# Side-by-side products for head pairs, and another order for the last output blocks, in a two-layer hybrid trunk

## Chip, cores and metric

The kernel runs on one NeuronCore of a Trainium2 chip. The metric is the device time of one launch in microseconds (us), from the first to the last instruction on the chip and what lies around them. Lower is better. Engines are named as in the profile: PE multiplies matrices (PEld is its loading of weights), DVE is the vector engine, ACT the scalar engine, POOL GpSimd, and SP issues the transfers.

## What is computed

Two layers, each on 512 tokens of width 1024. All in float32:

```
x <- x + 1/2 * SwiGLU_1(RMSNorm(x))              # 1024 -> 2 x 2816 -> 1024
h  = RMSNorm(x);  P = h @ W_in
y_A = RWKV-7 time mixing (8 heads of 64, decay and rate from rank-64 products, delta-rule state scan)
y_B = band attention (8 heads of 64, relative-position bias, softmax)
y_C = cross-attention into a memory of 256 tokens (4 heads of 128)
x <- x + W_out( sum_b sigmoid(h W_gate_b + b_gate_b) * (y_b @ W_branch_b) )
x <- x + 1/2 * SwiGLU_2(RMSNorm(x))
```

## The kernel before

Activations lie transposed: 128 channels on the partitions, 512 tokens along the row, so x is eight tiles `xs[0]` to `xs[7]`. A large product takes three half-precision (f16) matmuls for one in float32: weights and activations are split into a high and a low part, and `mm3` (line 714) adds high·high, high·low and low·high in PSUM. Each weight chunk is loaded by SP, measured and split by ACT and DVE (`load_w`, tile `wh`). Small products run in float32 directly; each float32 matmul has two records in the trace, one for each pass of it.

Nothing runs in the order in which it is written. Every operation is recorded (line 538 issues all of them, so all rows of the profile have that line), and `Plan.run` then lays the operations out on PE, DVE, ACT, POOL and SP with estimated costs and hands each engine a fixed order. Work on the longest remaining chain comes first; the f16 sums of large products fill PE between the small ones; matmuls recorded inside one `plan.block()` stay together. `plan.step(True)` makes the next large sum wait for the last one. Where the planner expects PE to stand idle for over 0.4 us it puts in matmuls on a tile of zeros (`xps<-wt`, 320 columns), which are called fills here; they keep PE's clock up, and their result is not used.

A layer has three parts. **First SwiGLU** (`ffn`): 22 blocks of the input projection, then output blocks; of an output chunk, the sums over the first 16 hidden blocks come from weights `w_a(n)` (one chunk of 128 outputs), those over the last 6 from `w_b(c)` (two chunks). `back` adds a sum to its `xs[n]`. For the last pair of chunks the second half of the sums is made for tokens 0 to 255 first, then for 256 to 511 (`HV`), so that the norm of the first half of the tokens, which the next part begins with, can start early. **Mixing** (`mixing`): projections, time mixing (`rwkv`), band attention (`band`), memory attention, gates and branches, and at its end `w_out`, in the last block also by halves. **Second SwiGLU**. A norm squares `xs[0]` to `xs[7]` on ACT, adds them up on DVE, and crosses the partitions by small matmuls (`s<-con,na` for the sum, `s<-con,rs` for the broadcast).

Places that the change touches, where 64-wide heads lie in pairs `u` = 0, 1 on partitions 0 to 63 and 64 to 127 (`H2`; `W2` is the two swapped):

- `soft` in `band`: for each of 4 pairs of heads, 4 blocks `b` of 128 queries and both `u`, a score product with 64 rows of contraction and (b+1)·128 keys (`as<-ak,aq`), into one of two PSUM tiles `a_ps()`; then bias, maximum, exponential and scaling on DVE and ACT, then `turn`, PE transposes of the result (`as<-con,sc`), which take a tile of the same two.
- `rwkv`, the products for decay and rate (`s<-xwa,lw`, 64 rows of contraction, 512 columns), one on each half of the partitions.
- `rwkv`, the output `yp` of each of 8 chunks of 64 tokens: for each `u` one product over 128 rows (`yp<-ar,gx`) and one over 64 (`yp<-kk,g` or `yp<-ta,g`), added in PSUM. This runs for 4 pairs of heads, 8 chunks and 2 layers. Ahead of it in each chunk stands the chain of the state, three pairs of products into `xps` (`xps<-ar,gx`, `xps<-cx,tt`, then `xps<-kk,kb` with `xps<-ta,be`), with DVE or ACT between them.

Of the kernel before, what the change touches and what calls it, by code (L numbers as in the profile page):

```python
# [10 lines left out]
AF = mybir.ActivationFunctionType  # L11
# [5 lines left out]
P = 128  # L17
DM = 1024
T = 512
DEPTH = 2  # L20
KT = DM // P
DFF = 2816
NH = DFF // P
NA = 16
MT = 256
CH = 64
# [529 lines left out]
def trunk(tc: tile.TileContext, i: dict, out: bass.AP, dbg: dict | None = None, depth: int = DEPTH):  # L556
# [47 lines left out]
    def s_ps():  # L604
        return pq.tile([P, T], F32, tag="s", name=nm("s"))

    def a_ps():
        return pa.tile([P, T], F32, tag="a", name=nm("as"))
# [188 lines left out]
    def ffn(l, f, g, d_h, start=(), body=()):  # L797
        start, body = iter(start), iter(body)
        with plan.pool(name=nm("fp"), bufs=30, reuse_waits="tile") as fp:
# [77 lines left out]
                w, d = load_w(i["ffn_outb"][l, f, c], (NH - NA) * 2 * P)  # L877
                return w.rearrange("p s (k n) -> p s k n", k=NH - NA), d

            for c in range(KT // 2):  # L880
                back(*w_a(2 * c), 0, 2 * c, 0, NA, dA)
                a, b = w_a(2 * c + 1), w_b(c)
                for c0, c1 in HV if c == KT // 2 - 1 else ((0, T),):
                    back(*a, 0, 2 * c + 1, 0, NA, dA, c0, c1)
                    for u in range(2):
                        back(*b, u, 2 * c + u, NA, NH, dB, c0, c1)
            plan.step(False)


# [81 lines left out]
    def mixing(l, pieces, kst):  # L971
# [106 lines left out]
        def band():  # L1078
            for p in range(NP):
                q_, k_, vt = att_of[p]  # L1080
                bias = ta_("bias", [P, 2, 2 * P])
                D.dma_start(out=bias, in_=i["bias"][l, p])
                V.memset(bias[0:CH, :, 2 * P - CH:2 * P], -1e30)
                sqs = []
                for t in (k_, q_):
                    sq = ta_("sc", bufs=3)
                    S.activation(sq, t, AF.Square)
                    sqs.append(sq)
                rs = []
                for sq in sqs:  # L1090
                    v = small("n8", 8)
                    V.tensor_scalar(out=v, in0=head_ss(sq, a_ps), scalar1=1.0 / CH, scalar2=1e-6, op0=ALU.mult, op1=ALU.add)
                    rs.append(rpow(v, 8))
                rq = small("rq", 8)
                V.tensor_scalar(out=rq, in0=rs[1], scalar1=CH ** -0.5, scalar2=None, op0=ALU.mult)
                V.scalar_tensor_tensor(out=k_, in0=k_, scalar=lv["aqk"], in1=head_bc(rs[0], a_ps), op0=ALU.mult, op1=ALU.mult)
                pt = []
                for u in range(2):
                    t = ta_("pt", [P, 1280], bufs=2)
                    pt.append([t[:, c0:c0 + T - b * P] for b, c0 in enumerate((0, 512, 896, 1152))])  # L1100

                def soft(b, u):
                    nk = (b + 1) * P
                    h = H2[u]
                    ps = a_ps()
                    PE.matmul(ps[:, :nk], lhsT=q_[h, b * P:(b + 1) * P], rhs=k_[h, 0:nk], start=True, stop=True)
                    sc = ta_("sc", bufs=3)
                    far = max(0, nk - 2 * P)
                    for c0, c1, bb in ((0, far, bias[:, u, 0:1].to_broadcast([P, far])), (far, nk, bias[:, u, 2 * P - (nk - far):2 * P])):
                        if c1 > c0:  # L1110
                            V.scalar_tensor_tensor(out=sc[:, c0:c1], in0=ps[:, c0:c1], scalar=rq[:, 2 * b + u:2 * b + u + 1], in1=bb, op0=ALU.mult, op1=ALU.add)
                    nx = small("nx")
                    V.tensor_reduce(out=nx, in_=sc[:, :nk], op=ALU.max, axis=AX.X, negate=True)
                    den = small("den")
                    S.activation(sc[:, :nk], sc[:, :nk], AF.Exp, bias=nx[:, 0:1], accum_out=den)
                    rd = small("rd")
                    V.reciprocal(rd, den)
                    V.tensor_scalar(out=sc[:, :nk], in0=sc[:, :nk], scalar1=rd[:, 0:1], scalar2=None, op0=ALU.mult)
                    return b, u, sc

                def turn(b, u, sc):
                    ps = a_ps()
                    with plan.block():
                        for kb in range(b + 1):
                            PE.transpose(ps[:, kb * P:(kb + 1) * P], sc[:, kb * P:(kb + 1) * P], ident)
                    for kb in range(b + 1):
                        S.activation(pt[u][kb][:, (b - kb) * P:(b - kb + 1) * P], ps[:, kb * P:(kb + 1) * P], AF.Copy)

                pend = []
                for b in range(4):  # L1130
                    for u in range(2):
                        pend.append(soft(b, u))
                        if len(pend) > 1:
                            turn(*pend.pop(0))
                turn(*pend.pop(0))
                ps = a_ps()
                with plan.block():
                    for kb in range(4):
                        for u in range(2):
                            PE.matmul(ps[H2[u], kb * P:T], lhsT=vt[:, kb, u * CH:(u + 1) * CH], rhs=pt[u][kb], start=(kb == 0), stop=(kb == 3))  # L1140
                y = tm("ya", bufs=5)
                S.activation(y, ps, AF.Copy)
                ya.append(y)
# [91 lines left out]
        def rwkv():  # L1235
            for p in range(NP):
# [14 lines left out]
                else:  # L1251
                    D.dma_start(out=vfs[p], in_=v_)

                ps = s_ps()
                PE.matmul(ps, lhsT=glob["lw"][0:CH, cs], rhs=glob["xwa"][0:CH, :], start=True, stop=True)
                tz = tr("w", bufs=3)
                S.activation(tz, ps, AF.Tanh, scale=0.5, bias=lv["w0"][:, p:p + 1])
                V.tensor_scalar(out=tz, in0=tz, scalar1=1.0, scalar2=None, op0=ALU.add)
                ps = s_ps()
                PE.matmul(ps, lhsT=glob["lw"][CH:P, cs], rhs=glob["xwa"][CH:P, :], start=True, stop=True)  # L1260
                ta = tr("ta")
                S.activation(ta, ps, AF.Tanh, scale=0.5, bias=lv["a0"][:, p:p + 1])
                cu = tr("w", bufs=3)
                V.tensor_tensor_scan(out=cu, data0=con[:, C_CM:C_CM + T], data1=tz, initial=0.0, op0=ALU.mult, op1=ALU.add)

# [111 lines left out]
                for c in range(NCH):  # L1377
# [24 lines left out]
                            else:  # L1402
                                S.activation(z, xp_[w, 2 * CH:3 * CH], AF.Copy, scale=aw[w, c:c + 1])
                    with plan.block():
                        for u, h in enumerate(H2):
                            o, w = yp[h, c * CH:(c + 1) * CH], W2[u]
                            PE.matmul(o, lhsT=gx[:, c, u, CH:2 * CH], rhs=vz[:, c, u, :], start=True, stop=False)
                            PE.matmul(o, lhsT=g1[w, c, :], rhs=vu[u][w, c, :], start=False, stop=True)


# [95 lines left out]
                put(mgd[k], acc[k], s)  # L1506
        for c2 in range(2):
            ws = [chunk(i["w_out"][l, 2 * c2 + c]) for c in range(2)]
            for c0, c1 in HV if c2 else ((0, T),):
                for (k0, k1), dx in zip(groups, dmg):  # L1510
                    for c in range(2):
                        w, d = ws[c]
                        dd = mul_d(d, dx)
                        for u in range(2):
                            n = 4 * c2 + 2 * c + u
                            plan.step(False)
                            ps = g_ps()[:, c0:c1]
                            mm3(ps, [(w[:, 0, k, u * P:(u + 1) * P], w[:, 1, k, u * P:(u + 1) * P], mgd[k][:, 0, c0:c1], mgd[k][:, 1, c0:c1]) for k in range(k0, k1)])
                            x = xs[n][:, c0:c1]
# [158 lines left out]
```

## Time and profile before

| | us |
|---|---|
| median of 3 runs | 2773.04 (2770.26 to 2778.02) |
| the profiled execution | 2773.73 |
| its span, first to last instruction | 2771.9 |
| PE busy | 2745.1 |
| DVE busy | 1626.2 |
| ACT busy | 1538.0 |

The rows further down are of this execution. A timeline row has the start, the length, the engine, the operation with output and inputs, partitions x elements, and how many instructions it merges. PE works in a pipe, so a row's length is longer than the time that it holds PE up; what one group of matmuls costs is the start of the next minus its own start.

### The profile page before, as it was taken

The page shows a single profiled execution, that of the slowest core. Times are in us where ns is not written, and L with a number is a line of the kernel's source. Part 1 is how long each engine was busy: PE and PEld are TensorE (multiplying, and loading weights), DVE is VectorE, ACT ScalarE, POOL GpSimd, SP SyncE. Part 2 cuts the span into 40 slices and gives each one's busy share as a digit, 9 for nine tenths or more (in the row PEclk, how much of TensorE's full clock was granted, in tenths as well). Part 3 has the DMA queues.
Part 4 walks back from the last instruction along what each step waited for, and adds up shares of the span by engine and source line. Part 5 has one row for each costly group of instructions (what it writes and reads, how often), then busy time and mean ns, then how long its engine had stood idle before and what let it go on. Part 6 is the DMA issues. An engine that isn't in the chain of part 4 may idle for free. (4 is left out here: it accounts for less than half of the span.)

```text
span 2771.9 us, 45458 instructions
## 1 busy us (share of the span) xinstructions
PE 2745.1 (99%) x18153; PEld 1496.6 (54%) x18153; DVE 1626.2 (59%) x4391; ACT 1538.0 (55%) x2543; POOL 111.1 (4%) x285
## 2 busy tenths in 40 slices
PE   9999999999999999999999999999999999999999
PEld 6444486565645456444564444765655454654445
DVE  6344486777766676354463544777776666743543
ACT  6556475565645566565455654655655445655652
POOL 0000000000000000000000000000000000000000
PEclk9999999999999999999999999999999999999999
DMA  4222341111121223222222223311212112232332
GB/s 169 105 93 103 122 140 69 51 61 45 52 83 70 85 98 115 95 104 99 99 107 105 93 106 118 129 52 42 70 35 75 67 54 92 92 114 100 107 106 77
DMA packets 47157, 249.36 MB, mean 90 GB/s; under 512 B 5312, under 2 KB 10688, under 8 KB 23648
## 3 DMA queue, kind: packets, MB, share of 16 engines
q1 hardware_dynamic: 46944, 246.45, 25.2%
q8 instruction: 142, 2.33, 0.3%
q14 instruction: 71, 0.58, 0.1%
HBM read 239.09 MB, written 7.34 MB: 89 GB/s over the span
## 5 line engine op out<-in xcount | busy, mean ns | idle before, releaser
L538 PEld LDWEIGHTS <-wh 128*128 128x128 f16 x10920 | 1047.6, 98 | 1008.0 <-issue 26.8
L538 PE MATMUL g<-hh,wh 128*128 128x512 f16 (+1 forms) x3216 | 987.0, 367 | 0.4 <-DVE k L538 0.4
L538 ACT ACTIVATE wh<-wr,qs 128x1024 f16<-128x1024 f32 (+2 forms) x478 | 484.0, 1050 | 222.5 <-PE g L538 114.3
L538 ACT ACTIVATE junk<-wr 128x2048 uint8<-128x2048 f32 (+2 forms) x239 | 412.9, 1727 | 332.9 <-DMA wr<-ffn_in 144.3
L538 PE MATMUL g<-hl,wh 128*128 128x512 f16 (+1 forms) x1608 | 588.9, 366 | 0.0
L538 DVE SCALAR_TENSOR_TENSOR wh<-wr,qs,wh 128x1024 f16<-128x1024 f32 (+2 forms) x478 | 545.2, 1168 | 43.8 <-ACT wh L538 42.9
L538 PE MATMUL as<-hh,wh 128*128 128x512 f16 (+1 forms) x1536 | 443.3, 361 | 0.0
L538 PE MATMUL as<-hl,wh 128*128 128x512 f16 (+1 forms) x768 | 277.4, 361 | 0.0
L538 PE MATMUL as<-ab,wh 128*128 128x512 f16 (+1 forms) x1224 | 234.7, 350 | 0.0
L538 PE MATMUL g<-ab,wh 128*128 128x512 f16 (+1 forms) x1224 | 234.5, 350 | 0.0
L538 POOL PARTITION_ALL_REDUCE ar<-wm x239 | 97.3, 407 | 2465.5 <-ACT junk L538 2313.6
L538 DVE SCALAR_TENSOR_TENSOR a<-as,md,sg 128x512 f32<-128x512 f32 x44 | 33.0, 750 | 213.3 <-PE as L538 210.0
L538 DVE SCALAR_TENSOR_TENSOR a<-g,md,sg 128x512 f32<-128x512 f32 x44 | 33.0, 750 | 212.9 <-PE g L538 202.7
L538 DVE SCALAR_TENSOR_TENSOR x<-g,md,x 128x512 f32<-128x512 f32 (+1 forms) x62 | 39.0, 628 | 115.8 <-PE g L538 115.8
L538 DVE SCALAR_TENSOR_TENSOR x<-as,md,x 128x512 f32<-128x512 f32 (+1 forms) x62 | 38.9, 628 | 115.8 <-PE as L538 115.8
L538 DVE TENSOR_SCALAR qt<-ar 128x1 int32<-128x1 int32 x253 | 37.6, 150 | 104.0 <-POOL ar L538 101.7
L538 ACT ACTIVATE sq<-x 128x256 f32<-128x256 f32 x96 | 37.0, 407 | 78.9 <-DVE x L538 50.6
L538 ACT ACTIVATE kk<-xps 64x64 f32<-64x64 f32 x64 | 14.0, 219 | 112.6 <-DVE ta L538 93.9
L538 ACT ACTIVATE ti<-s 64x256 f32<-64x256 f32 (+1 forms) x144 | 54.3, 378 | 28.2 <-PE s L538 18.3
L538 DVE SCALAR_TENSOR_TENSOR ab<-a,qs,ab 128x512 f16<-128x512 f32 x88 | 60.7, 746 | 10.3 <-ACT ab L538 10.3
L538 ACT ACTIVATE sg<-as,md 128x512 f32<-128x512 f32 x44 | 30.1, 684 | 56.2 <-PE as L538 56.2
L538 ACT ACTIVATE ab<-a,qs 128x512 f16<-128x512 f32 x88 | 55.9, 709 | 7.3 <-DVE qs L538 7.3
(345 smaller groups left out, 3133.4 us busy)
## 6 DMA issues: line engine op xcount, KB each, us to landing
wr<-ffn_in SPq DMA_DIRECT2D x88, 1024.0 KB, 4.8
wr<-ffn_outa SPq DMA_DIRECT2D x32, 1024.0 KB, 4.9
wr<-w_gate SPq DMA_DIRECT2D x24, 1024.0 KB, 4.9
wr<-w_in SPq DMA_DIRECT2D x22, 1024.0 KB, 4.9
wr<-ffn_outb SPq DMA_DIRECT2D x16, 768.0 KB, 4.3
wr<-w_branch SPq DMA_DIRECT2D x24, 512.0 KB, 3.5
wr<-mem_kv SPq DMA_DIRECT2D x8, 1024.0 KB, 4.9
wr<-w_out SPq DMA_DIRECT2D x8, 1024.0 KB, 4.8
```

Source lines behind the costliest of these rows:

```text
L538: f(*[x.real() if isinstance(x, View) else x for x in a], **{y: x.real() if isinstance(x, View) else x for y, x in k.items()})
```

## The change

It does five things. The two score products of a block `b` are recorded together in one `plan.block()`, before both softmaxes, and take both PSUM tiles. The decay and rate products are recorded in one block. In a chunk's output the two products over 128 rows come first, then the two over 64. In the last pair of chunks of SwiGLU's output the sums over the last 6 hidden blocks come first and whole, and then the two sums over the first 16, by halves of the tokens. In the last block of `w_out`, within a half, the sums go chunk by chunk and no longer group by group, and each waits for the last one (`plan.step(c2 == 1)`).

```diff
-            for c in range(KT // 2):
+            for c in range(KT // 2 - 1):
                 back(*w_a(2 * c), 0, 2 * c, 0, NA, dA)
                 a, b = w_a(2 * c + 1), w_b(c)
-                for c0, c1 in HV if c == KT // 2 - 1 else ((0, T),):
-                    back(*a, 0, 2 * c + 1, 0, NA, dA, c0, c1)
-                    for u in range(2):
-                        back(*b, u, 2 * c + u, NA, NH, dB, c0, c1)
+                back(*a, 0, 2 * c + 1, 0, NA, dA)
+                for u in range(2):
+                    back(*b, u, 2 * c + u, NA, NH, dB)
+            c += 1
+            b = w_b(c)
+            for u in range(2):
+                back(*b, u, 2 * c + u, NA, NH, dB)
+            ws = [w_a(2 * c + u) for u in range(2)]
+            for c0, c1 in HV:
+                for u in range(2):
+                    back(*ws[u], 0, 2 * c + u, 0, NA, dA, c0, c1)
...
-                def soft(b, u):
+                def scores(b):
                     nk = (b + 1) * P
-                    h = H2[u]
-                    ps = a_ps()
-                    PE.matmul(ps[:, :nk], lhsT=q_[h, b * P:(b + 1) * P], rhs=k_[h, 0:nk], start=True, stop=True)
+                    pss = [a_ps(), a_ps()]
+                    with plan.block():
+                        for ps, h in zip(pss, H2):
+                            PE.matmul(ps[:, :nk], lhsT=q_[h, b * P:(b + 1) * P], rhs=k_[h, 0:nk], start=True, stop=True)
+                    return pss
...
                 for b in range(4):
+                    pss = scores(b)
                     for u in range(2):
-                        pend.append(soft(b, u))
+                        pend.append(soft(b, u, pss[u]))
...
-                ps = s_ps()
-                PE.matmul(ps, lhsT=glob["lw"][0:CH, cs], rhs=glob["xwa"][0:CH, :], start=True, stop=True)
+                ps, ps2 = s_ps(), s_ps()
+                with plan.block():
+                    PE.matmul(ps, lhsT=glob["lw"][0:CH, cs], rhs=glob["xwa"][0:CH, :], start=True, stop=True)
+                    PE.matmul(ps2, lhsT=glob["lw"][CH:P, cs], rhs=glob["xwa"][CH:P, :], start=True, stop=True)
...
-                        for u, h in enumerate(H2):
-                            o, w = yp[h, c * CH:(c + 1) * CH], W2[u]
+                        ys = [yp[h, c * CH:(c + 1) * CH] for h in H2]
+                        for u, o in enumerate(ys):
                             PE.matmul(o, lhsT=gx[:, c, u, CH:2 * CH], rhs=vz[:, c, u, :], start=True, stop=False)
+                        for u, (o, w) in enumerate(zip(ys, W2)):
                             PE.matmul(o, lhsT=g1[w, c, :], rhs=vu[u][w, c, :], start=False, stop=True)
...
-            for c0, c1 in HV if c2 else ((0, T),):
-                for (k0, k1), dx in zip(groups, dmg):
-                    for c in range(2):
+            order = [(0, T, g, c) for g in range(2) for c in range(2)]
+            if c2:
+                order = [(c0, c1, g, c) for c0, c1 in HV for c in range(2) for g in range(2)]
...
-                            plan.step(False)
+                            plan.step(c2 == 1)
```

Since the planner orders everything anew, the change moves instructions far beyond these lines. Three places on PE, the first of each kind in the program, before and then after.

A chunk's output in `rwkv` of layer 0 (`yp`), with the matmuls next to it. Before:

```order
L538 MATMUL xps<-kk_5163,kb_1014_4121 64x64
L538 MATMUL xps<-ta_5081,be_4783 64x64
L538 MATMUL yp_294<-ar_4769,gx_4124 64x64
L538 MATMUL yp_294<-kk_5163,g_1002_4125 64x64
L538 MATMUL yp_294<-ar_4769,gx_4124 64x64
L538 MATMUL yp_294<-ta_5081,g_1002_4125 64x64
L538 LDWEIGHTS wh_4912
```

The two products of one head stood together, and then those of the other. After:

```order
L538 MATMUL g_5593<-wh_5497,hl_2570 128x128
L538 MATMUL yp_294<-ar_4771,gx_4163 64x64 x2
L538 MATMUL yp_294<-kk_5194,g_1000_4164 64x64
L538 MATMUL yp_294<-ta_5103,g_1000_4164 64x64
L538 LDWEIGHTS hh_2571
```

Now the products of the two heads that have one shape are neighbours.

The scores of the first pair of heads in `band`, layer 0, block b = 1 (`as<-ak,aq`, 256 keys); `g` rows are f16 sums of a projection. Before, with most rows between the two heads left out:

```order
L538 MATMUL g_5188<-wh_5146,hl_2570 128x128
L538 MATMUL as_5305<-ak_4151,aq_4153 128x256
L538 LDWEIGHTS hh_2571
...
L538 MATMUL as_5393<-ak_4151,aq_4153 128x256
L538 MATMUL as_5392<-con,sc_5023 128x128
```

The second head's product came much later than the first's. After:

```order
L538 MATMUL xps<-kk_5194,kb_1012_4160 64x64
L538 MATMUL xps<-ta_5103,be_4785 64x64
L538 MATMUL as_5235<-ak_4190,aq_4192 128x256
L538 MATMUL as_5295<-ak_4190,aq_4192 128x256
L538 MATMUL xps<-ar_4771,gx_4163 64x64 x2
```

Now the two stand next to each other.

The end of `w_out` in layer 0, ahead of the second SwiGLU: `as` and `g` are the last sums, `s<-con,na` crosses the partitions for the norm of a half of the tokens, `s<-con,rs` spreads its result, and `xps<-wt` are fills. Before:

```order
L538 MATMUL s_10173<-con,na_11161 128x1 x2
...
L538 MATMUL s_10185<-con,rs_3747 128x128 x2
...
L538 MATMUL as_11265<-ti_9718,wh_10963 128x256
L538 LDWEIGHTS wt
L538 MATMUL xps<-wt 128x320
...
L538 MATMUL s_11206<-con,na_11363 128x1 x2
```

The first half's two crossings stood among the last sums; 26 fills followed the last sum, then the second half's crossing. After:

```order
L538 MATMUL s_10312<-con,na_11185 128x1 x2
...
L538 MATMUL g_11265<-ti_9831,wh_11039 128x256
L538 LDWEIGHTS wt
L538 MATMUL xps<-wt 128x320
...
L538 MATMUL s_10322<-con,rs_3733 128x128 x2
...
L538 MATMUL s_11296<-con,na_11408 128x1 x2
```

The first half's spread has moved behind the last sum: 28 fills stand ahead of it, and 14 more between it and the second half's crossing.

## Rows read from the trace of the kernel before

**Rows 1.** The page: span, busy time and share of each engine, and the granted TensorE clock in 40 slices (9 is 90% or more).

```profile
span 2771.9 us, 45458 instructions
PE 2745.1 (99%) x18153; PEld 1496.6 (54%) x18153; DVE 1626.2 (59%) x4391; ACT 1538.0 (55%) x2543; POOL 111.1 (4%) x285
PEclk9999999999999999999999999999999999999999
```

**Rows 2.** Busy time of each engine by stage: the stretch, its length, then busy us (instructions) of each engine, granted clock, share of DMA and GB/s. The stretches are mixing of layer 0, its gates and w_out, the two SwiGLUs between, mixing of layer 1.

```profile
430.00:930.00 500.00, 490.83 (x4309) 280.74 (x4306) 350.40 (x1060) 267.25 (x567) 15.61 (x41) 1.00 0.17 60
930.00:1040.00 110.00, 110.00 (x614) 59.89 (x613) 75.28 (x188) 69.73 (x104) 5.96 (x16) 1.00 0.28 101
1040.00:1790.00 750.00, 750.00 (x4048) 396.05 (x4046) 372.13 (x886) 419.96 (x585) 31.62 (x80) 1.00 0.30 107
1790.00:2300.00 510.00, 501.23 (x4348) 284.26 (x4346) 357.97 (x1067) 275.39 (x576) 15.96 (x40) 1.00 0.17 59
```

**Rows 3.** Timeline of PE: the decay and rate products of one pair of heads where they happened to stand together, and one such product alone.

```profile
421.60 1.13 PE L538 MATMUL s<-xwa,lw 64*128 64x512 f32 x4
422.67 0.39 PE L538 MATMUL g<-hh,wh 128*128 128x512 f16 x1
...
542.48 0.38 PE L538 MATMUL g<-hh,wh 128*128 128x512 f16 x1
542.78 1.12 PE L538 MATMUL s<-xwa,lw 64*128 64x512 f32 x2
543.84 0.39 PE L538 MATMUL g<-hh,wh 128*128 128x512 f16 x1
```

**Rows 4.** Timeline of PE: score products of both heads together (128 keys), and of one head alone (256, 384 and 512 keys), each with the row behind it.

```profile
489.24 0.49 PE L538 MATMUL as<-ak,aq 64*128 64x128 f32 x4
489.66 0.28 PE L538 MATMUL g<-wh,hh 128*128 128x128 f16 x2
...
492.36 0.70 PE L538 MATMUL as<-ak,aq 64*128 64x256 f32 x2
492.99 0.29 PE L538 MATMUL g<-wh,hh 128*128 128x128 f16 x2
...
557.91 0.91 PE L538 MATMUL as<-ak,aq 64*128 64x384 f32 x2
558.75 0.39 PE L538 MATMUL g<-hh,wh 128*128 128x512 f16 x1
...
507.09 1.12 PE L538 MATMUL as<-ak,aq 64*128 64x512 f32 x2
508.14 0.44 PE L538 MATMUL as<-con,sc 128*128 128x128 f32 x2
```

**Rows 5.** Timeline of PE: the first record of the last step of a chunk's state chain, the same chunk's output in `rwkv`, and the row behind it.

```profile
496.84 0.27 PE L538 MATMUL xps<-kk,kb 128*64 128x64 f32 x1
...
497.01 0.28 PE L538 MATMUL yp<-ar,gx 128*64 128x64 f32 x2
497.22 0.33 PE L538 MATMUL yp<-kk,g 64*64 64x64 f32 x2
497.48 0.33 PE L538 MATMUL yp<-ar,gx 128*64 128x64 f32 x2
497.74 0.33 PE L538 MATMUL yp<-ta,g 64*64 64x64 f32 x2
497.99 0.28 PE L538 MATMUL g<-wh,hh 128*128 128x128 f16 x2
```

**Rows 6.** Timeline of PE and DVE: two steps of a chunk's state chain, each with both heads' products as neighbours, and the DVE copy between them.

```profile
617.57 0.34 PE L538 MATMUL xps<-ar,gx 128*64 128x64 f32 x4
617.83 1.12 PE L538 MATMUL as<-ak,aq 64*128 64x512 f32 x2
617.95 0.22 DVE L538 COPY cx<-xps 128x64 f32<-128x64 f32 x1
...
618.88 0.33 PE L538 MATMUL xps<-cx,tt 64*64 64x64 f32 x4
619.15 0.39 PE L538 MATMUL g<-hh,wh 128*128 128x512 f16 x1
```

**Rows 7.** Fills: the matmuls on the tile of zeros in all (count, then shortest, median and longest record in ns, first and last start in us, forms), and two groups of them on PE's timeline with the rows behind them; a row of which PE waited for something would end in brackets.

```profile
L538 PE MATMUL xps<-wt x337: 296/299/474, 1.0 to 2439.7; 128*128 128x320 f16 x169
...
1039.43 3.74 PE L538 MATMUL xps<-wt 128*128 128x320 f16 x26
1043.02 0.50 PE L538 MATMUL s<-con,na 128*128 128x1 f32 x4
...
1396.58 2.23 PE L538 MATMUL xps<-wt 128*128 128x320 f16 x15
1398.65 0.27 PE L538 MATMUL g<-hh,wh 128*128 128x256 f16 x1
```

**Rows 8.** Timeline of DVE and ACT: the softmax of one head's block of 128 queries and 512 keys, whose score product ended PE's part at 583.97 us (bias in two pieces, maximum, exponential, scaling).

```profile
584.08 0.88 DVE L538 SCALAR_TENSOR_TENSOR sc<-as,rq,bias 128x256 f32<-128x256 f32 x2 [1.15 <-PE as L538]
...
584.99 0.69 DVE L538 TENSOR_REDUCE nx<-sc 128x1 f32<-128x512 f32 x1
...
585.71 0.72 ACT L538 ACTIVATE sc<-sc,nx 128x512 f32<-128x512 f32 x1 [1.30 <-DVE nx L538]
...
586.77 0.49 DVE L538 TENSOR_SCALAR sc<-sc,rd 128x512 f32<-128x512 f32 x1
```

More of the change, by code (lines that the diff above doesn't have):

```diff
@@ L1100, in band, with soft @@
                     pt.append([t[:, c0:c0 + T - b * P] for b, c0 in enumerate((0, 512, 896, 1152))])
-                def soft(b, u):
+                def scores(b):
                     nk = (b + 1) * P
-                    h = H2[u]
-                    ps = a_ps()
-                    PE.matmul(ps[:, :nk], lhsT=q_[h, b * P:(b + 1) * P], rhs=k_[h, 0:nk], start=True, stop=True)
+                    pss = [a_ps(), a_ps()]
[3 more added lines that the diff above has]
+                    return pss
+                def soft(b, u, ps):
+                    nk = (b + 1) * P
                     sc = ta_("sc", bufs=3)
@@ L1258, in rwkv @@
                 V.tensor_scalar(out=tz, in0=tz, scalar1=1.0, scalar2=None, op0=ALU.add)
-                ps = s_ps()
-                PE.matmul(ps, lhsT=glob["lw"][CH:P, cs], rhs=glob["xwa"][CH:P, :], start=True, stop=True)
                 ta = tr("ta")
-                S.activation(ta, ps, AF.Tanh, scale=0.5, bias=lv["a0"][:, p:p + 1])
+                S.activation(ta, ps2, AF.Tanh, scale=0.5, bias=lv["a0"][:, p:p + 1])
                 cu = tr("w", bufs=3)
@@ L1508, in mixing @@
             ws = [chunk(i["w_out"][l, 2 * c2 + c]) for c in range(2)]
-            for c0, c1 in HV if c2 else ((0, T),):
-                for (k0, k1), dx in zip(groups, dmg):
-                    for c in range(2):
-                        w, d = ws[c]
-                        dd = mul_d(d, dx)
-                        for u in range(2):
+            order = [(0, T, g, c) for g in range(2) for c in range(2)]
+            if c2:
+                order = [(c0, c1, g, c) for c0, c1 in HV for c in range(2) for g in range(2)]
+            for c0, c1, g, c in order:
+                    (k0, k1), dx = groups[g], dmg[g]
+                    w, d = ws[c]
+                    dd = mul_d(d, dx)
+                    for u in range(2):
                             n = 4 * c2 + 2 * c + u
-                            plan.step(False)
+                            plan.step(c2 == 1)
                             ps = g_ps()[:, c0:c1]
```

## The prediction

> **What bounds the kernel now.** I read the page first: PE is busy for 2745.1 of 2771.9 us, at full granted clock in every slice, and DVE and ACT for little over half [rows 1]. So PE's idle time is 26.8 us in all, under 1%. The table by stage says where: gates, w_out and the two SwiGLUs have none, the two mixing stages have 9.2 and 8.8 us [rows 2]. DVE is the next engine there, with 350.4 of 500 us. Nothing can be won by starting PE earlier; what counts is how long its queue is, and that is what the change touches. The sum below is therefore PE's queue, term by term, plus what it waits.
>
> A busy PE isn't a useful one, though: 337 of its matmuls are fills [rows 7], and they belong to the queue too.
>
> **Two products side by side.** A timeline shows what two products cost that use different halves of the partitions. At 421.60 the decay and rate products stand together, four records, and PE goes on 1.07 us later; the one at 542.78 alone takes 1.06 us [rows 3]. Two cost what one costs. In the order of before 2 of 8 such pairs are neighbours already; the other 6 save 6 x 1.06 = **6.4 us**.
>
> Scores: a head alone takes 0.63, 0.84 and 1.05 us for 256, 384 and 512 keys; the two of 128 keys are neighbours already, 0.42 us for both [rows 4], in all 8 pairs of heads (4 in each layer). The other three blocks are apart in all 8. I take the second product as free, as in rows 3: 8 x (0.63 + 0.84 + 1.05) = **20.2 us** saved.
>
> Output of a chunk: now 497.99 - 497.01 = 0.98 us [rows 5]. No row has it in the new order, but rows 6 have both of its halves in form. Two products over 128 rows, into the two halves of PSUM's partitions, take 0.26 us (617.57 to 617.83); two over 64 rows, one on each half, take 0.27 us (618.88 to 619.15). So 0.53 us, 0.45 us less, for 4 x 8 x 2 = 64 chunks: **28.8 us** saved. The ends: a pair that is followed by another of its form holds PE for only 0.17 us (496.84 to 497.01) [rows 5], which would save 0.09 x 64 = 6 us more; and if nothing overlapped, nothing would be saved. I take 0.53, since the second pair has another form than the first, as what follows the pair at 617.57 has.
>
> Together PE's queue gets 55.4 us shorter. Places where PE goes from f16 to float32 work are 477 in the order before and 485 after, so I count nothing for changing over.
>
> **What the new order adds.** The order of after holds 555 fills, 218 more. A fill costs 3.59 us / 26 = 0.138 us at 1039.43 and 2.07 / 15 = 0.138 at 1396.58, and behind neither group does PE wait further [rows 7]; the fills were enough, so each added one is time in the queue, whether the gap it was meant for is real or not: 218 x 0.138 = **30.1 us** added. By place, from the two orders: the start 116 and 116; the norms ahead of and behind the SwiGLUs 87 and 87; the ends of w_out 103 and 151; inside mixing 31 and 201.
>
> That settles the two reorderings of last blocks. For SwiGLU's output the fills stay the same, so I cost it at nothing: it makes 48 more matmuls, each half as wide, and the columns are the same. Its weights come in another order on SP's queue (w_b ahead of the two w_a), and of the two `wh` buffers both are held to the end, as before; the SwiGLU stages have PE at 750.00 of 750.00 us [rows 2], which is the cover. For w_out the new order costs 48 x 0.138 = 6.6 us (in the 30.1): with each sum waiting for the last, xs[2] and xs[3] get their last addend behind the first sums of the last block, the squares of a norm run in the order of xs, and so the first half's norm ends behind the last sum.
>
> **Waits.** PE reaches the next step of a state chain 0.45 us sooner in each chunk. In rows 6 the copy that the second step reads ends at 618.17, and PE gets there at 618.88: 0.71 us, more than it loses. If that held nowhere, 64 x 0.45 = 29 us would come back. In the other direction, the fills that were put in for products costed apart may cover waits that are there now, of which mixing has 18 us; I bound that at -8. I take +3, near the row's end.
>
> **The sum.** 2771.9 - 55.4 + 30.1 + 3 = 2749.6 us of span. The profiled execution is 1.8 us longer than its span, and the median is 0.7 us under it, so **2751 us**, 0.8% faster.
>
> **Rivals.** *The softmaxes fall behind (slower).* A pair of scores takes both `as` tiles. Before, one head's scores could go ahead while the other's transposes held the second tile; now the pair waits on its engine until the last transposes are copied out, and the whole of PE's queue waits behind it. A head's softmax takes from 583.97 to 587.26, 3.3 us [rows 8]. If each of the 24 pairs of over 128 keys leaves PE with 1.5 us of it, that is 36 us, and 2787 us; it decides from 24 / 24 = 1.0 us for each pair. For it: the order of after has fills ahead of transposes and head sums of band and memory attention. Against: between a pair and its first head's transposes that order has 12 to 78 f16 matmuls besides other work, which at the rows' rates is 3 us or more each time, and DVE has 30% of the stage free.
>
> *DVE is late more often.* The same work of 350.4 us in a stage that is 10 to 20 us shorter; PE waits 13 us more than I take, 2764 us.
>
> *The 64-row pair of a chunk's output takes turns.* Both write one PSUM tile, `yp`. If they went one after the other at 0.26 and 0.25 us [rows 5], the block would take 0.77 us and the change would save 0.21 x 64 = 13 us on it: 2766 us. Against it: `xps<-cx,tt` writes one PSUM tile from both halves of the partitions as well, and its four records take 0.27 us [rows 6]. The Trainium skill has this as a rule (TensorEngine Tiling (Array Packing), section Restrictions and Gotchas): different row tiles cannot access the same PSUM bank at the same time. By that rule 2766 us would be right; the trace disagrees with it, with the 0.27 us just named.
>
> *It doesn't do what it says for the outputs.* Accumulating pairs might not overlap at all, since no row has a pair that opens a sum and a second pair that adds to it: 28.8 us less saved, 2780 us.
>
> *More than the forecast.* Fills cover present waits (-8), and the outputs come at 0.44 us (-6): about 2738 us.
>
> **How the numbers follow.** Forecast 0.58; more than it 0.12; DVE late 0.12; taking turns 0.04; no overlap of outputs 0.05; softmaxes behind 0.09. A measurement of this kernel can tell about 0.3% from no change, 8.3 us: faster is under 2764.7, slower over 2781.4. Faster: 0.58 + 0.12 + half of 0.12 = 0.76. Same: the other half, 0.04 and 0.05 = 0.15. Slower: 0.09. The range runs from 2738 to 2770: it leaves out the softmaxes, the outputs without overlap and some 0.05 at the low end.
>
> **What would show it.** Right: `s<-xwa,lw` and `as<-ak,aq` rows of x4 that hold PE for one product's time; a chunk's output in about 0.53 us; 555 fills with no wait behind most groups; mixing some 22 us shorter in layer 0 and 10 in layer 1 (27.7 saved in each, less 44 and 126 fills), and each end of w_out 3 us longer. Wrong: PE idle in mixing well over 18 us, most of all ahead of `as<-ak,aq` or `as<-con,sc` (softmaxes), or ahead of `xps` rows (state chain), or a chunk's output of 0.77 or 0.98 us.

## The result, and the profile after

The changed kernel takes 2755.35 us (median of 4 runs, 2751.40 to 2756.55); the kernel before took 2773.94 us beside it (4 runs, 2770.26 to 2778.02). The ratio is 0.9930 [0.9913, 0.9948], where the brackets hold a 95% interval: 0.7% faster. The forecast was 2751 us. The profiled execution took 2755.16 us.

The page of the changed kernel, with the lines that answer to [rows 1]:

```profile
span 2753.3 us, 45958 instructions
PE 2720.2 (99%) x18419; PEld 1491.8 (54%) x18419; DVE 1621.1 (59%) x4383; ACT 1539.8 (56%) x2543; POOL 111.2 (4%) x285
PEclk9999999999999999999999999999999999999999
```

The span is 18.6 us shorter. PE is busy for 24.9 us less, and its idle time has grown from 26.8 to 33.1 us, so 6.3 us came back as waits. The table by stage of the changed kernel, for the two mixing stages (columns as in [rows 2]; the stretches follow the work, which is earlier now):

```profile
410.00:910.00 500.00, 488.96 (x4442) 278.92 (x4439) 358.14 (x1083) 276.47 (x581) 15.71 (x43) 0.99 0.18 63
1770.00:2275.00 505.00, 490.68 (x4447) 279.30 (x4446) 357.94 (x1078) 280.46 (x584) 17.28 (x43) 1.00 0.17 62
```

The waits are where they were, in mixing: 11.0 and 14.3 us. In layer 0 the granted clock is 0.99 now; it was 1.00.

PE's timeline of the changed kernel at five places: a pair of scores of 512 keys, the end of `w_out` in layer 0, two chunks' outputs, a pair of rate products, and a wait in layer 1 that the order before doesn't have. A bracket is the time that PE stood idle ahead of a row.

```profile
556.64 1.13 PE L538 MATMUL as<-ak,aq 64*128 64x512 f32 x4
557.71 0.39 PE L538 MATMUL g<-hh,wh 128*128 128x512 f16 x1
...
1020.46 4.02 PE L538 MATMUL xps<-wt 128*128 128x320 f16 x28
1024.31 0.60 PE L538 MATMUL s<-con,rs 128*128 128x128 f32 x4
1024.76 2.09 PE L538 MATMUL xps<-wt 128*128 128x320 f16 x14
1026.68 0.50 PE L538 MATMUL s<-con,na 128*128 128x1 f32 x4
1027.05 1.95 PE L538 MATMUL xps<-wt 128*128 128x320 f16 x13
1028.83 0.27 PE L538 MATMUL as<-hh,wh 128*128 128x256 f16 x1
...
1869.54 0.34 PE L538 MATMUL yp<-ar,gx 128*64 128x64 f32 x4
1869.81 0.27 PE L538 MATMUL yp<-kk,g 64*64 64x64 f32 x1
1869.82 0.27 PE L538 MATMUL yp<-ta,g 64*64 64x64 f32 x1
...
1870.07 0.34 PE L538 MATMUL yp<-ar,gx 128*64 128x64 f32 x4
...
2046.49 1.13 PE L538 MATMUL s<-xwa,lw 64*128 64x512 f32 x4
2047.55 1.98 PE L538 MATMUL as<-pt,mv 128*128 128x512 f32 x4
...
2054.19 1.40 PE L538 MATMUL xps<-wt 128*128 128x320 f16 x9
2058.36 0.38 PE L538 MATMUL g<-hh,wh 128*128 128x512 f16 x1 [2.76 <-DVE r L538]
```

Two scores of 512 keys hold PE for 557.71 - 556.64 = 1.07 us, where one alone took 1.05 [rows 4]; two rate products take 1.06. A chunk's output takes 1870.07 - 1869.54 = 0.53 us; the one of [rows 5] took 0.98, and one without a pair of products right ahead of it took 1.03 (rows under "The pairs in the queue"). The two 64-row products that add to `yp` start 0.01 us apart. All these pairs run side by side.

The fills of the changed kernel (columns as in [rows 7]):

```profile
L538 PE MATMUL xps<-wt x555: 296/299/474, 1.0 to 2409.2; 128*128 128x320 f16 x185
```

Where PE's time went can be added up. The table takes, over each whole trace, the time from the start of each PE row to the start of the next, less all time in between in which PE was idle (a bracket shows it where it is over 0.15 us), and adds these times by kind, in us. The last column is the changed kernel with its fills left out (below). The last row is the mean granted clock of the execution.

| PE's time by kind | before | changed | outputs alone | scores alone | three pairs | changed, no fills |
|---|---|---|---|---|---|---|
| waits behind the first matmul | 21.9 | 28.4 | 22.4 | 32.4 | 30.1 | 72.9 |
| fills (count) | 50.9 (337) | 81.9 (555) | 51.0 (337) | 62.3 (422) | 71.2 (476) | 0 |
| chunk outputs | 63.1 | 32.0 | 31.2 | 63.8 | 32.0 | 31.7 |
| scores | 43.8 | 23.9 | 43.8 | 24.4 | 23.8 | 23.8 |
| rate products | 14.7 | 8.9 | 14.7 | 14.7 | 8.5 | 9.8 |
| other float32 | 350.0 | 351.1 | 349.3 | 357.8 | 352.2 | 361.9 |
| f16 | 2222.6 | 2222.5 | 2222.7 | 2226.8 | 2221.5 | 2242.1 |
| mean granted clock | 0.999 | 0.998 | 0.999 | 0.995 | 0.998 | 0.990 |

From before to changed: outputs -31.1, scores -19.9, rates -5.8, fills +31.0, waits +6.5, the rest +1.0; in all -18.3 us.

### The profile page after: what moved, and what is told of

It reads as the page before. It is cut to its first block, busy times and chain, and to the rows that moved or that the text cites. A ratio compares the mean times of both kernels' runs of the same rounds, so it can differ in the third digit from the quotient of the medians.

```text
span 2753.3 us, 45958 instructions
## 1 busy us (share of the span) xinstructions
PE 2720.2 (99%) x18419; PEld 1491.8 (54%) x18419; DVE 1621.1 (59%) x4383; ACT 1539.8 (56%) x2543; POOL 111.2 (4%) x285
## 5 line engine op out<-in xcount | busy, mean ns | idle before, releaser
L538 PEld LDWEIGHTS <-wh 128*128 128x128 f16 x10968 | 1051.7, 98 | 1006.8 <-issue 31.1
L538 PE MATMUL g<-hh,wh 128*128 128x512 f16 (+2 forms) x2704 | 822.5, 365 | 2.8 <-DVE r L538 2.8
L538 PE MATMUL as<-hh,wh 128*128 128x512 f16 (+1 forms) x2048 | 609.2, 366 | 0.1
L538 PE MATMUL g<-hl,wh 128*128 128x512 f16 (+2 forms) x1352 | 492.4, 364 | 0.0
L538 PE MATMUL as<-hl,wh 128*128 128x512 f16 (+1 forms) x1024 | 374.5, 366 | 0.0
L538 DVE SCALAR_TENSOR_TENSOR a<-g,md,sg 128x512 f32<-128x512 f32 x88 | 66.0, 750 | 437.9 <-PE g L538 429.6
L538 ACT ACTIVATE sg<-as,md 128x512 f32<-128x512 f32 x88 | 60.2, 684 | 115.8 <-PE as L538 115.8
L538 PE MATMUL xps<-wt 128*128 128x320 f16 x555 | 88.2, 309 | 1.0 <-DVE wt L538 1.0
L538 PEld LDWEIGHTS <-wt 128*128 128x128 f16 x555 | 55.7, 102 | 26.0 <-issue 1.9
L538 DVE SCALAR_TENSOR_TENSOR ab<-a,qs,ab 128x512 f16<-128x512 f32 x88 | 60.7, 746 | 10.4 <-ACT ab L538 10.4
L538 ACT ACTIVATE pt<-as 128x128 f32<-128x128 f32 (+1 forms) x176 | 42.5, 312 | 39.4 <-PE as L538 38.8
```

What stands on the lines that cost most here:

```text
L538: f(*[x.real() if isinstance(x, View) else x for x in a], **{y: x.real() if isinstance(x, View) else x for y, x in k.items()})
```

## The experiments

Every ratio is against the kernel before, run beside it. The first three take the change apart.

**The outputs alone.** To the kernel before only this was done; the order of all other work and the 337 fills stay as they were:

```diff
-                        for u, h in enumerate(H2):
-                            o, w = yp[h, c * CH:(c + 1) * CH], W2[u]
+                        ys = [yp[h, c * CH:(c + 1) * CH] for h in H2]
+                        for u, o in enumerate(ys):
                             PE.matmul(o, lhsT=gx[:, c, u, CH:2 * CH], rhs=vz[:, c, u, :], start=True, stop=False)
+                        for u, (o, w) in enumerate(zip(ys, W2)):
                             PE.matmul(o, lhsT=g1[w, c, :], rhs=vu[u][w, c, :], start=False, stop=True)
```

> The kernel before with one part alone: in a chunk's output the two products over 128 rows first, then the two over 64. The planner's order and its 337 fills stay as before. Theory (PE's queue sets the time, pairs run side by side): 64 chunks x 0.45 to 0.49 us shorter, 28 to 31 us, so 2743 to 2747 us against 2774. Rival (the state chain takes the time back, PE only waits longer ahead of xps): less than 15 us saved, 2759 us or more.

Measured: 2741.78 us, 0.9888 [0.9872, 0.9905], some 12 us under the changed kernel by the ratios, 13.6 by the times. One of the five edits, without the other four, is the fastest version that was run. PE's timeline of it at the chunk of [rows 5]:

```profile
495.21 0.27 PE L538 MATMUL xps<-kk,kb 128*64 128x64 f32 x1
...
495.38 0.29 PE L538 MATMUL yp<-ar,gx 128*64 128x64 f32 x4
495.60 0.27 PE L538 MATMUL yp<-kk,g 64*64 64x64 f32 x1
...
495.86 0.29 PE L538 MATMUL g<-wh,hh 128*128 128x128 f16 x2
```

Here the output takes 0.48 us, less than 0.53, since it stands right behind a pair of its own form (`xps<-kk,kb` with `xps<-ta,be`). The waits are 22.4 us against 21.9: PE comes to the next step of a state chain half a microsecond earlier, and the step's operands are there.

**All three pairs, without the two orders of last blocks.** The changed kernel, with these two loops put back:

```diff
-            for c in range(KT // 2 - 1):
+            for c in range(KT // 2):
...
-            order = [(0, T, g, c) for g in range(2) for c in range(2)]
...
+            for c0, c1 in HV if c2 else ((0, T),):
...
-                            plan.step(c2 == 1)
+                            plan.step(False)
```

> The changed kernel with both last-block orders undone: only the three pair edits. Its order has 476 fills, 139 more than before. Theory: 57 us of pairs less, 139 x 0.14 = 19 us of fills more, some 5 us of waits more: 33 us less than before, 2741 us, and so 14 us less than the changed kernel. Rival (the gain comes from the halves of the last blocks): no different from before, 2774 us, and slower than the changed kernel.

Measured: 2745.75 us, 0.9898 [0.9884, 0.9913]. The two orders of last blocks cost the changed kernel some 9 us. But scores and rates, 26 us shorter in PE's queue by the table, give nothing beyond the outputs: the fills take 20.2 us more than in the kernel of the outputs alone, the waits 7.7.

**The two orders of last blocks alone**, on the kernel before:

```diff
+            order = [(0, T, g, c) for g in range(2) for c in range(2)]
+            if c2:
+                order = [(c0, c1, g, c) for c0, c1 in HV for c in range(2) for g in range(2)]
...
-                            plan.step(False)
+                            plan.step(c2 == 1)
```

and likewise SwiGLU's loop in its new form.

> The kernel before with the two last-block orders alone (SwiGLU's output and w_out). Its order has 482 fills, 145 more than before. Theory: these orders bring nothing and the fills cost 145 x 0.14 = 20 us: 2794 us, slower by 0.7%. Rival (the halves of the last blocks are what gains): 2765 us or less.

Measured: 2799.50 us, 1.0099 [1.0084, 1.0115]: slower by 1%, some 27 us, with 482 fills instead of 337. In the changed kernel the same two orders cost some 9 us. What an edit costs thus depends on the order that it is planned into, and the prices of the five edits don't simply add up.

**Are the gaps real that fills are put into?** The changed kernel with the same order, but no fill issued (their result is used nowhere):

```diff
-                        out.append(w)
+                        pass
```

> The changed kernel with the same order on every engine, but none of the 555 fills issued (the planner still reckons with them). If the gaps are real, PE waits in place of the fills: about 2755 us, or some more where a long wait lets TensorE's clock fall. If the fills are waste, all but the 116 at the start go: up to 439 x 0.14 = 61 us less, 2694 us. My theory of the prediction said only that a fill is time in the queue either way, so it is open which; the trace's waits at the places of the fills tell it apart place by place.

Measured: 2760.55 us, 0.9954 [0.9939, 0.9968], 5 us above the changed kernel. The rival, by which fills are wasted queue time, falls. The table shows it: 81.9 us of fills go, 44.5 us of waits come, another 9.3 us pass ahead of the first matmul, and everything else takes 31 us more (f16 alone 19.6). So about two thirds of the fills' time came back as standing. Of the 31 us the clock is a large part: 0.990 against 0.998 over 2756 us is some 22 us, an estimate that takes PE as never idle; the rest the table doesn't tell apart. PE's timeline without fills, at the end of `w_out` in layer 0:

```profile
1024.33 0.71 PE L538 MATMUL s<-con,rs 128*128 128x128 f32 x4 [3.44 <-DVE rs L538]
1026.74 0.98 PE L538 MATMUL s<-con,na 128*128 128x1 f32 x4 [1.70 <-DVE na L538]
```

and the table by stretch of the same kernel around it:

```profile
1000.00:1040.00 40.00, 32.74 (x269) 27.28 (x267) 35.89 (x116) 25.96 (x46) 1.96 (x4) 0.91 0.30 102
```

`s<-con,rs` starts at 1024.33, with 28 fills ahead of it at 1024.31: the fills ended when the data came. The crossing takes 0.98 us instead of 0.50, at a granted clock of 0.91 in the stretch.

**The same with the kernel before**, the same edit:

> The kernel before, same order on every engine, none of its 337 fills issued. Without fills the changed kernel got 5 us slower: 82 us of fills went, 44 us came back as waits and some 31 us as TensorE's slower clock. If the gaps behind the fills are as real in the order of before: 2773 to 2780 us. If its fills are waste: 2745 us.

Measured: 2773.61 us, 0.9998 [0.9989, 1.0007]. Its 50.9 us of fills were replaced by 31.7 of waits (9.9 of them ahead of the first matmul), and the rest takes 19 us more. The mean granted clock, 0.996 against 0.999, is worth some 8 of these 19 us; as far as the granted clock shows, the expectation put too much of such time down to it. In sum, leaving the fills out neither costs nor brings time there.

**The scores' pair alone**, on the kernel before:

```diff
+                    pss = [a_ps(), a_ps()]
+                    with plan.block():
+                        for ps, h in zip(pss, H2):
+                            PE.matmul(ps[:, :nk], lhsT=q_[h, b * P:(b + 1) * P], rhs=k_[h, 0:nk], start=True, stop=True)
...
-                    ps = a_ps()
-                    PE.matmul(ps[:, :nk], lhsT=q_[h, b * P:(b + 1) * P], rhs=k_[h, 0:nk], start=True, stop=True)
```

> The kernel before with the score pairs alone. Its order has 422 fills, 85 more than before. Queue theory: 20 us less for the 24 pairs, 85 x 0.14 = 12 us more for fills, some 4 us more of waits: about 2769 us against 2773, no clear difference. Rival (the pairs' gain is real and the added fills are an accident that other waits would have filled): 2755 us.

Measured: 2792.62 us, 1.0072 [1.0059, 1.0084]. This was a miss: 20 us slower. The scores do get 19.4 us shorter; fills take 11.4 us more, waits 10.5, and the other work 12 us more. That is the profiled execution, the fastest of five with 2788.70 us and a clock of 0.995; the others had 0.991 to 0.994 and took 2792.42 us or more. The greatest wait, on PE's and DVE's timeline of this kernel:

```profile
1933.33 0.92 PE L538 MATMUL as<-ak,aq 64*128 64x384 f32 x4
1934.10 0.33 DVE L538 TENSOR_SCALAR sc<-sc,rd 128x256 f32<-128x256 f32 x1
...
1938.69 0.74 DVE L538 SCALAR_TENSOR_TENSOR sc<-as,rq,bias 128x256 f32<-128x256 f32 x2
...
1939.58 0.66 PE L538 MATMUL as<-con,sc 128*128 128x128 f32 x2 [4.58 <-DVE rs L538]
1940.03 0.63 PE L538 MATMUL g<-hh,wh 128*128 128x512 f16 x1
1940.46 0.63 PE L538 MATMUL g<-hl,wh 128*128 128x512 f16 x1
```

The two transposes `as<-con,sc` of the 256-key block are for the second head. Their input `sc` was scaled at 1934.10 and done by 1934.43. They still start at 1939.58, behind DVE's reading of the first head's next scores (1938.69 to 1939.43); `rs` in the bracket is only the small operation that DVE ended last. Why is read from the code, since no row names the tile: `turn` takes the next `as` tile, there are two, and the pair at 1933.33 holds both until DVE has added the bias. DVE did thirteen other operations first. The table by stretch of this kernel, for the wait and behind it:

```profile
1936.00:1939.00 3.00, 0.00 (x0) 0.00 (x0) 2.94 (x10) 0.00 (x0) 0.00 (x0) 0.84 0.70 238
1939.00:1950.00 11.00, 10.42 (x59) 5.26 (x59) 8.39 (x27) 5.24 (x13) 0.38 (x1) 0.73 0.08 32
```

PE is idle in the first stretch with DVE busy for 2.94 of 3 us, and then runs at a mean granted clock of 0.73, with f16 rows 0.43 us apart. So the wait is paid for more than once: 4.58 us of standing, and up to 3 us (0.27 x 11) of slow clock.

**The two tiles without the pair.** Both scores recorded ahead of both softmaxes, as above, but without `plan.block()`, so the planner may part them:

```diff
-                    with plan.block():
+                    if True:
```

> As the run with score pairs alone, but the two products are recorded one after the other without a block, so that only the order of recording and of taking the two PSUM tiles is new; 14 of 32 pairs are neighbours in its order (32 of 32 with the block, 8 before), and it has 411 fills, 74 more than before. If taking both tiles at once is what delays the softmaxes: 74 x 0.14 = 10 us more for fills, 5 us less for the 6 new neighbours, 4 us more of waits, about 2782 us. If the block is what delays them: no slower than before, 2773 us or less.

Measured: 2780.47 us, 1.0027 [1.0018, 1.0035], as expected. The scores get 6.1 us shorter (14 of 32 pairs stand together), the fills 10.4 us longer, the waits 1.3. The price of recording both scores early and taking both tiles is thus some 14 us (7.7 slower, although the scores got 6.1 shorter), against some 39 with the block (19.9 and 19.4), about a third. The block makes the kernel 12 us slower, though its scores are 13 us shorter: 9.2 us more waits, and 12 more of float32 and f16 work. Those 12 are about what the clock costs: its mean was 0.999 without the block and 0.995 with it, some 11 us over 2787.

**The changed kernel with `w_out`'s order put back**, SwiGLU's new order kept:

```diff
-            order = [(0, T, g, c) for g in range(2) for c in range(2)]
-            if c2:
-                order = [(c0, c1, g, c) for c0, c1 in HV for c in range(2) for g in range(2)]
...
-                            plan.step(c2 == 1)
+                            plan.step(False)
```

> The changed kernel with the order of w_out alone put back: three pair edits and the new order of SwiGLU's output. 485 fills against 555. Theory: 70 x 0.14 = 10 us less than the changed kernel, 2746 us, the same as with both last orders undone. Rival (SwiGLU's new order is what cost): no less than the changed kernel, 2755 us.

Measured: 2746.09 us, 0.9901 [0.9886, 0.9916], against 0.9930 of the changed kernel: `w_out`'s order costs 8 to 9 us. Its PE timeline at the end of `w_out` in layer 0:

```profile
1023.32 3.74 PE L538 MATMUL xps<-wt 128*128 128x320 f16 x26
1026.90 0.50 PE L538 MATMUL s<-con,na 128*128 128x1 f32 x4
1027.26 0.98 PE L538 MATMUL xps<-wt 128*128 128x320 f16 x6
1028.09 0.27 PE L538 MATMUL as<-hh,wh 128*128 128x256 f16 x1
```

From the first fill behind the last sum to the first product of SwiGLU it takes 4.77 us; in the changed kernel 1028.83 - 1020.46 = 8.37. Twice 3.60 is 7.2 us of the 8 to 9. It is the same in layer 1 (4.77 and 8.38 us). The wait of 2.76 us ahead of `g<-hh,wh` is found in kernels with `w_out`'s new order (1.69 us in the one with last blocks alone) and not in this one, but it doesn't explain the price: this kernel has a wait of 2.39 us at 2110.12 instead, and waits for 29.8 us in all, against 28.4.

**Outputs and SwiGLU's new order**, on the kernel before (the outputs' edit above, and SwiGLU's loop in its new form):

> The kernel before with the chunk outputs in pairs and the new order of SwiGLU's output, nothing else. 332 fills, 5 fewer than before. Theory: SwiGLU's order costs nothing and brings nothing but its fills, 5 x 0.14 = 0.7 us: 2741 us, the same as the chunk outputs alone (2742). Rival (the new order of SwiGLU's output lets the norm start sooner): 2736 us or less.

Measured: 2742.86 us, 0.9891 [0.9877, 0.9904], against 0.9888 of the outputs alone. SwiGLU's order does nothing, in this kernel as in the one above (0.9901 with it, 0.9898 without).

**Is the planner's reckoning at fault?** It counts both products of a pair in full. In the kernel with the three pairs, the second product of a score or rate pair is now told as free:

```diff
-        o.us += self.cost(o, eng, name, outs[0], ins, k)
+        o.us += 0.0 if self.beside(o, eng, name, k) else self.cost(o, eng, name, outs[0], ins, k)
```

(`beside` is true for the second float32 product of a block with at most 64 rows and 128 columns of weights.)

> The three pair edits (last-block orders undone), with one thing more: the planner is told that the second product of a score pair or rate pair costs nothing, where it counts two. 474 fills against 476. If PE waits for softmaxes and its clock falls because the planner lays out work for two products where one product's time passes, then the waits go from 30 to some 22 us and the falls of the clock go too: 2736 us against 2746. Rival (a pair takes both PSUM tiles and the softmaxes are late whatever the planner reckons): no better, 2746 us.

Measured: 2750.15 us, 0.9914 [0.9901, 0.9928]; not better than 0.9898 without it. The fills stay (474, against 476) and PE waits 34.1 us instead of 30.1. The theory that the planner only had wrong costs falls.

**Other orders for the pairs.** `LIFT` is what the planner adds to the due time of `rwkv`'s operations (110 in all kernels so far). Outputs and rate pairs, without the scores' pair, at 112; and all three pairs at 111:

```diff
-LIFT = 110
+LIFT = 112
```

> The kernel before with the chunk outputs and the rate products in pairs, scores as before, last blocks as before; the constant LIFT is 112 in place of 110, which leaves 352 fills (387 with 110). Queue theory: 31 and 6 us less, 15 x 0.14 = 2 us more: 2738 us, some 4 us under the chunk outputs alone. If rate pairs bring waits as score pairs do: 2745 us.

> All three pair edits, last blocks as before, LIFT 111 in place of 110, which leaves 421 fills (476 with 110). Queue theory: 55 x 0.14 = 8 us less than with 476: 2738 us. If the waits for softmaxes are what eats the score pairs' gain and not the fills: 2746 us or more.

Measured: 2749.42 us, 0.9916 [0.9903, 0.9930], a miss, and 2747.40 us, 0.9902 [0.9887, 0.9917], where the rival held. (One of the latter's five executions took 6219.25 us, for which nothing here shows the cause; the ratio is without it.) Neither beats the outputs alone. The first has 352 fills, only 15 more than before, and waits of 27.3 us, and still doesn't get there. Its profiled execution shows one reason in the table by stretch:

```profile
600.00:609.00 9.00, 6.15 (x101) 5.02 (x100) 6.72 (x36) 2.53 (x4) 0.39 (x1) 1.00 0.33 117
609.00:633.00 24.00, 24.00 (x96) 11.10 (x97) 19.19 (x66) 13.01 (x34) 0.74 (x2) 0.50 0.13 45
```

After 9 us in which PE stood idle for 2.85, it worked without a pause for 24 us at the lower level of its clock (0.50 is 1.2 GHz), which is 12 us lost. That execution took 2756.69 us, the others of this kernel 2747.96 to 2750.06. The others have no trace, but their mean granted clock was 0.995 as well, against 0.999 for the outputs alone: some 11 us by the same estimate, where they are 6 to 8 us slower than the outputs alone. So the slow clock is there in each execution, and the count of fills doesn't show it.

The rate pair was never run by itself with `LIFT` at 110, so its own price is not known.

## Why the prediction was right, and where its sizes were off

**What bounds the kernel.** Right: PE's queue does. Taking 31 us out of it with the order left as it was brought 31 us. What the sum left out is the clock (below).

**The pairs in the queue.** Right in all three forms: scores -19.9 (forecast -20.2), rates -5.8 (-6.4). The outputs' term was mis-sized: -31.1 against -28.8. The step that failed took the 0.98 us of [rows 5], a chunk with a pair of products right ahead of it, and set against it the 0.53 us of a chunk without one. PE's timeline of the kernel before has chunks without one too:

```profile
651.37 0.38 PE L538 MATMUL g<-hh,wh 128*128 128x512 f16 x1
651.67 0.33 PE L538 MATMUL yp<-ar,gx 128*64 128x64 f32 x2
...
652.70 0.70 PE L538 MATMUL s<-xg,gw 128*128 128x512 f32 x1
```

It took 652.70 - 651.67 = 1.03 us. Like with like, it is 0.98 to 0.48 and 1.03 to 0.53: 0.50 us saved in each kind, where the forecast had 0.45. The rivals of taking turns and of no overlap fall with the rows at 1869.81 and 1869.82: two products over different 64 rows of the array, both adding to one `yp` tile, and a block of 0.53 us where taking turns would need 0.77. The rule that the prediction took from the Trainium skill (TensorEngine Tiling (Array Packing), Restrictions and Gotchas) doesn't hold for these two, which write different partitions of that tile.

**Fills.** Right: 555, +31.0 us against +30.1. That "each added one is time in the queue" held for these kernels, since leaving the fills out brought nothing in either. But they are not simply waste: some two thirds of their time came back as waits, and the rest as slower work.

**The last blocks.** SwiGLU's at nothing: right. `w_out`'s at 6.6: it is 8 to 9 us. 70 fills depend on it, not 48: the changed kernel has 555 fills against 485 with the order put back, and 70 x 0.138 = 9.7 us.

**Waits.** Mis-sized: +6.5, where I took +3. The step was about the state chain, and the chain as a whole didn't mind (outputs alone: +0.5). Two single waits that the order before doesn't have come to 5.1 us: 2.76 us at 2058.36, which goes with `w_out`'s order, and 2.30 us in layer 0. PE's and DVE's timeline of the changed kernel around the second:

```profile
612.35 1.66 DVE L538 SCALAR_TENSOR_TENSOR sc<-as,rq,bias 128x256 f32<-128x256 f32 x4 [1.11 <-PE as L538]
...
613.92 1.27 DVE L538 TENSOR_REDUCE nx<-sc 128x1 f32<-128x512 f32 x2
...
617.29 1.26 DVE L538 SCALAR_TENSOR_TENSOR wh<-wr,qs,wh 128x1024 f16<-128x1024 f32 x1
617.33 0.34 PE L538 MATMUL xps<-ar,gx 128*64 128x64 f32 x4
...
619.52 0.88 DVE L538 TENSOR_SCALAR sc<-sc,rd 128x512 f32<-128x512 f32 x2
620.43 0.23 DVE L538 COPY cx<-xps 128x64 f32<-128x64 f32 x1
620.71 0.48 PE L538 MATMUL xps<-cx,tt 64*64 64x64 f32 x4 [2.30 <-DVE cx L538]
```

The two heads' scores come at once, so DVE has both softmaxes in hand at once: bias x4, maxima x2, scaling x2, where [rows 8] show one head's. The copy `cx`, whose input PE had written by 617.67, starts at 620.43, behind a split of weights, two other products and both scalings; in [rows 6] it started 0.38 us behind `xps<-ar,gx`, here 3.1 us. The scalings are 0.88 us of that, so the softmaxes are a part of the delay and the weights another. It doesn't follow from the pairs alone: the kernel with the three pairs and the old last blocks has no wait over 0.15 us ahead of `xps<-cx,tt`, and its longest is 2.29 us at 2108.78, ahead of `as<-con,pt`. The table by stretch of the changed kernel, ahead of that wait and behind it:

```profile
612.00:620.00 8.00, 5.88 (x89) 3.17 (x87) 7.51 (x16) 6.37 (x15) 0.00 (x0) 1.00 0.20 44
620.00:628.00 8.00, 7.29 (x34) 3.71 (x36) 2.30 (x13) 3.77 (x13) 0.38 (x1) 0.57 0.15 57
```

DVE is busy for 7.51 of 8 us, then PE runs at a mean of 0.57 of its clock for 8 us, up to 3.4 us lost (0.43 x 8). A term for the clock was missing in the prediction. It cost the changed kernel little in the end (0.998 against 0.999), since its first 30 us had a mean clock of 0.94 and those of the kernel before 0.89. The scores alone had 0.995, some 11 us.

**By place.** The crossing ahead of SwiGLU that started at 1043.02 in [rows 7] now starts at 1026.68, 16.3 us earlier, and the last one at 2402.3 instead of 2421.5, 19.2 us earlier. I had forecast 22 - 3 = 19 for layer 0 and 10 - 3 = 7 for layer 1; it was 16.3, with all that comes ahead of it, and 2.9. PE's time added up as in the table, but by layer, shows the difference. In layer 0 the pairs, fills and waits came out close to the forecast, and other float32 work took 3.0 us longer; the slow clock behind 620.71 lies there. In layer 1 the waits grew by 5.4 us.

**The rivals.** "The softmaxes fall behind" had a chance of 9% for the whole change, and didn't decide it. For the scores' edit by itself the time came out on its side: 20 us slower, with a wait of 4.58 us on a tile that the pair holds. But that wait and the slow clock behind it are some 8 us; 11.4 us of fills and the other falls of the clock are the larger part. I had looked for PE waiting ahead of the pair; it waits behind it, at the transposes, and the place named in the last part ("ahead of `as<-con,sc`") was the right one. The total came out near the forecast in part by luck: the outputs brought 31 us instead of 28.8, and the other four edits together lost 12 to 14 us, where their terms in the sum (-20.2 - 6.4 + 30.1 + 3) make 6.5. The two errors have opposite signs.

What stays open: how much of the scores' price is the tiles and how much the order in which DVE gets its work. A third `as` tile would tell; it wasn't tried. Nor was the rate pair by itself.

## What to carry to other kernels

Two products on different halves of TensorE's rows or columns took little more time here than one (1.07 against 1.05 us for scores of 512 keys, 0.27 against 0.21 for the 128-row products of an output). So first put those side by side that are neighbours already: here it changed no order and took nothing early. A pair that must be brought together can hold two buffers from the first product on, and give its consumer twice the work at once, as the scores did; price that by who needs the next buffer, and test each edit of a change by itself, since here one edit brought all of the gain and the others together gave some of it back. Where a planner fills gaps, the number of fills in a new order is a first estimate of the standing in it ahead of any run, but no more: forecasts from it missed by 11 us for the rate pairs at `LIFT` 112 and by 24 for the scores alone, both kernels with a mean clock of 0.995 or less.

## What was not expected of the hardware

A single wait of 2.30 us (at 620.71, above), with PE busy for 5.88 of the 8 us before, was followed by 8 us at a mean granted clock of 0.57. And once the clock was low it could stay at 0.50 for 24 us of uninterrupted work (609 to 633 in the kernel at `LIFT` 112), in one execution that took 7 to 9 us more than the others of that kernel.

A chunk's output of two pairs takes 0.53 us, but 0.48 where a pair of the first one's form stands right ahead of it: what a pair costs depends on the pair before it.
